# Forgetting attention with the gate sums in the mask, two heads' scores in alternating order, and squares on ScalarE

## The chip, the core and the metric

The kernel runs on one core of a Trainium2 chip. The metric is device time in microseconds, from the start of the program to its end, taken over several runs. A change is also looked at through a profile of one execution, which lists every instruction of the engines: PE (TensorE) with its weight loads PEld, DVE (VectorE), ACT (ScalarE), POOL (GpSimd), and SP, whose queue issues the DMA transfers.

## The reference

A model of four layers for one sequence of 256 tokens and width 1024 in float32. The first layer puts 16 meta tokens in front (272 positions) and mixes them by two groups of eight attention heads each, MLA (latent) and forgetting attention. The change concerns the forgetting heads, whose mathematics is this (B = 1, dimension 64, causal):

```
qf = rms_norm(fq, g_q_fox);  kf = rms_norm(fk, g_k_fox);  vf = fv
log_f = log_sigmoid(f_logit + b_forget)
F = cumsum(log_f over positions)                # one sum per head and position
s[q, k] = qf[q] . kf[k] * 64**-0.5 + F[q] - F[k]
p = softmax(where(k <= q, s, -1e30));  o = p @ vf
```

F[q] is the same for all keys of a query, so it falls out of the softmax; -F[k] does not. All other layers (a short convolution, a differential attention, an mLSTM, four squared-ReLU MLPs) are the same in both kernels.

## The kernel before, in words

**Stream and precision.** All weight matrices lie in one stream of 128x128 tiles. `Weights._ensure` (L82 to L100) loads 16 tiles (1 MB) at a time into one of three buffers `raw` on SP's queue (L86), and splits four tiles at a time into a rounded part `whi` on ACT (L92) and a rest `wlo` on DVE (L95; while `shared` is set, every third on POOL). `mm3` (L176) does each product as three f32r matmuls (L179 to L181). A matmul whose operands are plain f32 is issued as two instructions.

**Order.** [...] `queue_behind` (L67) adds an order between two instructions without a wait. [...]

**The attention layer** (`attention`, L343). `latent_proj` and `latent_norm` (L358, L375) make the two latents; `latent_norm` squares its chunks on POOL (L380) and adds them there (L384), sums over partitions on PE (L385), and applies the inverse root on DVE (L391) before a split into the operands `g_ckv` and `g_cq`. A mixed group gives the shared rotary key `kp` (its square `sqpe` L416 and its scaling L417, both on POOL) and the forget logits, from which `log_sigmoid_setup` and a scan (L424) make `cum`, the sums F as 8 rows of 272. L426 to L440 build from it the operands of a gate product: `fq` (F in two parts and ones, in 32-row groups), `fk` (ones and -F) and `hot` (one-hot columns), zeros elsewhere.

`fox_groups` (L449) projects the forgetting queries and keys, two heads to a tile of 128 rows: copy out of PSUM on ACT (L454), square on POOL (L456), gain on POOL (L458). `fox_norm` (L460) sums the squares per head by L464 on PE and writes the inverse roots to DRAM; `fox_scale` (L670) reads them back broadcast and multiplies on POOL (L676). Three of the eight tiles come early (at 34 to 47 us), five after the MLA queries. The MLA keys get their norm through DRAM as well: `kapd` (L490), then a broadcast for each head (`kt`, L515), on SP's queue; L649 needs them.

`minis` (L560) treats the last two meta tokens as queries (2 rows, 16 keys); `pair(j, ...)` (L595) treats the 256 others for the heads 2j and 2j + 1. For each head e a PSUM bank from a pool of two (`stile`) takes two score blocks, 128 queries by 144 keys and 128 by 272. `v.tensor_tensor_reduce` (L612) adds the causal mask, scales and takes the extreme; ACT takes the exponential (L615); DVE normalises (L617 to L621); PE transposes (L623 to L625); ACT copies (L627); the products with the values (L637, L641, L642) go into one bank, the two heads in its two halves of 64 partitions; `split` makes the operands of the output projection. The projection's first half needs the MLA heads only and lies between the forgetting pairs; the second half follows them.

The scores differ by group. MLA has L649 and L650 over 128 rows. For a forgetting head `fox_mm` (L652) adds two products in PSUM: L654 over the head's 64 rows (rows 0 to 63 for even heads, 64 to 127 for odd ones) and L655, the gate product over 128 rows with `fkh`, which is `fk` masked to this head on POOL (L662). For the small scores the masked copy is `fkm` (L667).

Of the kernel before, what the change touches and what calls it, by code (L numbers as in the profile page):

```python
# [6 lines left out]
F32 = mybir.dt.float32  # L7
F32R = mybir.dt.float32r
AF = mybir.ActivationFunctionType
# [5 lines left out]
P = 128  # L15
# [51 lines left out]
def queue_behind(tc, later, earlier):  # L67
# [3 lines left out]
        reason="issue order")  # L71

# [53 lines left out]
class Model:  # L126
# [216 lines left out]
    def attention(self, hv):  # L343
        with ExitStack() as c2:
# [30 lines left out]
            def latent_norm(cs, gain, n):  # L375
                nch = len(cs)
                pst = self.xtile(n)
                for c in range(nch):
                    q = self.tmp("latsq", n, width=T)
                    g.tensor_tensor(out=q, in0=cs[c], in1=cs[c], op=ALU.mult)  # L380
# [35 lines left out]
            g.tensor_tensor(out=sqpe[64:], in0=kp[64:], in1=kp[64:], op=ALU.mult)  # L416
            g.tensor_tensor(out=kp[64:], in0=kp[64:], in1=tabk[64:], op=ALU.mult)  # L417
# [8 lines left out]
            fq = ap.tile([P, T], F32R, name="fq")  # L426
            fk = ap.tile([P, T], F32, name="fk")
            hot = ap.tile([P, 8], F32, name="hot")
            g.memset(fq.bitcast(F32), 0.0)
            g.memset(fk, 0.0)  # L430
            g.memset(hot, 0.0)
            for r in (0, 32, 64, 96):
                g.tensor_copy(hot[r:r + 8], ident[0:8, 0:8])
            for r in (0, 32):
                g.tensor_copy(fk[r:r + 8], self.onesrow)
                g.tensor_copy(fq[64 + r:72 + r], self.onesrow)
            v.tensor_copy(fq[0:8], cum)
            v.tensor_tensor(out=fq[32:40], in0=cum, in1=fq[0:8].bitcast(F32), op=ALU.subtract)
            for r in (0, 32):
                v.tensor_scalar(out=fk[64 + r:72 + r], in0=fq[r:r + 8].bitcast(F32), scalar1=-1.0, scalar2=None, op0=ALU.mult)  # L440
# [8 lines left out]
            def fox_groups(js):  # L449
                for j in js:  # L450
# [3 lines left out]
                    s.activation(out=fraw[j], in_=pt, func=AF.Copy)  # L454
                    fsq[j] = self.tmp("sq8", n, bufs=8, width=T)
                    g.tensor_tensor(out=fsq[j], in0=fraw[j], in1=fraw[j], op=ALU.mult)  # L456
                    gain = self.vec("gk_fox") if j >= 4 else self.gqf8
                    g.tensor_scalar(out=fraw[j], in0=fraw[j], scalar1=gain, scalar2=None, op0=ALU.mult)  # L458
# [101 lines left out]
            def minis(score, scale, banks):  # L560
# [6 lines left out]
                for e in range(2):  # L567
# [6 lines left out]
                    else:  # L574
                        v.tensor_copy(sv[:, :, e], pm_)
# [17 lines left out]
            mask = self.cst("maskb")  # L593

            def pair(j, score, scale, vals, mini, oc):  # L595
# [6 lines left out]
                px = []  # L602
# [54 lines left out]
            def score_fox_mini(dst, h):  # L657
                fox_mm(dst, h, 14, 16, 16, fkm[:, h])
# [654 lines left out]
```

## Time and profile before

| | us |
|---|---|
| median of 3 runs (1237.07 to 1240.48) | 1238.38 |
| the profiled execution, its own time | 1238.09 |
| span of that execution, first to last instruction | 1236.3 |
| PE busy / PEld busy | 1214.4 / 1166.9 |
| DVE busy / ACT busy / POOL busy | 890.6 / 740.0 / 175.0 |

The granted TensorE clock is 0.997 of full speed in the mean. Busy times are shares of the whole span, over stages with different limits. Matmuls are pipelined, so the distance from one start to the next tells more of what one costs than its listed duration does. A merged row of the time line (x2, x4) has the first start and the time from there to the last end. What ended an idle time is inferred from semaphore events.

### The profile page before, as it was taken

The page shows a single profiled execution, that of the slowest core. Times are in us where ns is not written, and L with a number is a line of the kernel's source. Part 1 is how long each engine was busy: PE and PEld are TensorE (multiplying, and loading weights), DVE is VectorE, ACT ScalarE, POOL GpSimd, SP SyncE. Part 2 cuts the span into 40 slices and gives each one's busy share as a digit, 9 for nine tenths or more (in the row PEclk, how much of TensorE's full clock was granted, in tenths as well). Part 3 has the DMA queues.
Part 4 walks back from the last instruction along what each step waited for, and adds up shares of the span by engine and source line. Part 5 has one row for each costly group of instructions (what it writes and reads, how often), then busy time and mean ns, then how long its engine had stood idle before and what let it go on. Part 6 is the DMA issues. An engine that isn't in the chain of part 4 may idle for free.

```text
span 1236.3 us, 24763 instructions
## 1 busy us (share of the span) xinstructions
PE 1214.4 (98%) x9628; PEld 1166.9 (94%) x9628; DVE 890.6 (72%) x1792; ACT 740.0 (60%) x1518; POOL 175.0 (14%) x218
## 2 busy tenths in 40 slices
PE   8999999999999999999999999999999999999996
PEld 7787789999999999999998999999999989999996
DVE  7786668766567787766557888776558888876553
ACT  5655557764555567755446666775447665776452
POOL 5543330001101120001001011000100313000110
PEclk9999999999999999999999999999999999999998
DMA  7343126545455454554564435555555534554551
GB/s 279 121 173 105 52 98 219 182 174 200 172 178 197 171 196 181 181 195 171 189 212 147 156 118 184 192 175 190 183 179 186 184 135 157 189 200 171 189 187 35
DMA packets 35417, 210.15 MB, mean 170 GB/s; under 512 B 4642, under 2 KB 9940, under 8 KB 10852
## 3 DMA queue, kind: packets, MB, share of 16 engines
q1 hardware_dynamic: 34628, 207.98, 47.8%
q8 instruction: 76, 1.25, 0.4%
q10 hardware_dynamic: 576, 0.52, 0.1%
q14 instruction: 41, 0.34, 0.1%
q0 software_dynamic: 96, 0.06, 0.0%
HBM read 207.45 MB, written 1.10 MB: 169 GB/s over the span
## 4 chain that ended last, share of the span: by engine, by line
PE 93%; DVE 4%; DMA 1%; ACT 1%; issue 0%; POOL 0%; SPq 0%; DVEq 0%; ACTq 0%
PE d L179 26%; PE d L180 26%; PE d L181 26%; PE s L179 1%; DVE wlo L95 1%; PE s L180 1%; PE s L181 1%; PE d L336 1%; PE d L337 1%; PE d L338 1%; PE s L654 1%; DVE xl L201 1%; DMA kapd<-row 0%; PE y L179 0%; DVE ht L317 0%
## 5 line engine op out<-in xcount | busy, mean ns | idle before, releaser
L92 ACT ACTIVATE whi<-raw 128x512 fp32r<-128x512 f32 x768 | 478.7, 630 | 361.3 <-PE d L180 320.8
L95 DVE TENSOR_TENSOR wlo<-raw,whi 128x512 fp32r<-128x512 f32 x763 | 540.0, 713 | 211.6 <-ACT whi L92 194.5
L180 PE MATMUL d<-xl,whi 128*128 128x256 f32 (+2 forms) x1472 | 418.1, 285 | 2.4 <-DVE xl L201 2.4
L179 PE MATMUL d<-xh,whi 128*128 128x256 f32 (+2 forms) x1472 | 416.9, 284 | 2.0 <-DVE ht L317 1.6
L181 PE MATMUL d<-xh,wlo 128*128 128x256 f32 (+2 forms) x1472 | 414.1, 282 | 0.0
L181 PE MATMUL d<-uh,wlo 128*128 128x256 f32 (+1 forms) x1024 | 289.9, 283 | 0.0
L179 PE MATMUL d<-uh,whi 128*128 128x256 f32 (+1 forms) x1024 | 289.6, 283 | 0.0
L180 PE MATMUL d<-ul,whi 128*128 128x256 f32 (+1 forms) x1024 | 289.3, 282 | 0.0
L180 PEld LDWEIGHTS d<-xl,whi 128*128 128x128 f32 x1472 | 277.8, 189 | 4.7 <-DVE xl L201 3.0
L179 PEld LDWEIGHTS d<-xh,whi 128*128 128x128 f32 x1472 | 277.3, 189 | 5.2 <-ACT whi L92 2.9
L181 PEld LDWEIGHTS d<-xh,wlo 128*128 128x128 f32 x1472 | 279.1, 190 | 1.1 <-issue 0.3
L179 PEld LDWEIGHTS d<-uh,whi 128*128 128x128 f32 x1024 | 196.1, 191 | 0.0
L180 PEld LDWEIGHTS d<-ul,whi 128*128 128x128 f32 x1024 | 196.1, 191 | 0.0
L181 PEld LDWEIGHTS d<-uh,wlo 128*128 128x128 f32 x1024 | 195.6, 191 | 0.0
L252 POOL TENSOR_TENSOR acc<-ht 128x256 f32<-128x256 f32 (+1 forms) x8 | 5.3, 663 | 449.6 <-DVE ht L317 449.6
L260 POOL TENSOR_TENSOR acc<-sq,acc 128x256 f32<-128x256 f32 (+1 forms) x48 | 44.8, 934 | 139.7 <-ACT sq L257 137.8
L198 DVE TENSOR_TENSOR ul<-q,uh 128x256 fp32r<-128x256 f32 (+1 forms) x128 | 54.1, 425 | 11.5 <-ACT uh L197 0.2
L304 DVE SCALAR_TENSOR_TENSOR u<-d,rs 128x256 f32<-128x256 f32 (+1 forms) x116 | 48.9, 424 | 18.1 <-PE d L181 17.7
L197 ACT ACTIVATE uh<-q 128x256 fp32r<-128x256 f32 (+1 forms) x128 | 53.0, 416 | 3.4
L306 ACT ACTIVATE q<-u 128x256 f32<-128x256 f32 (+1 forms) x128 | 52.7, 415 | 0.0
L317 DVE TENSOR_TENSOR ht<-d,ht 128x256 f32<-128x256 f32 (+1 forms) x74 | 30.3, 420 | 18.8 <-PE d L181 18.8
L201 DVE SCALAR_TENSOR_TENSOR xl<-ht,vecs,xh 128x256 fp32r<-128x256 f32 (+2 forms) x64 | 41.2, 654 | 0.3 <-ACT xh L200 0.3
(425 smaller groups left out, 1516.9 us busy)
## 6 DMA issues: line engine op xcount, KB each, us to landing
raw<-in_wstream_dram SPq DMA_DIRECT2D x191, 1024.0 KB, 4.8
ht<-in_xt_dram SPq DMA_DIRECT2D x8, 136.0 KB, 4.0
kt<-kapd SPq DMA_DIRECT2D x8, 136.0 KB, 3.5
raw<-in_wstream_dram SPq DMA_DIRECT2D x4, 256.0 KB, 4.3
bt<-brd SPq DMA_DIRECT2D x8, 128.0 KB, 3.3
consts<-in_consts_dram SPq DMA_DIRECT2D x1, 556.0 KB
fbc<-kfd SPq DMA_DIRECT2D x8, 68.0 KB, 2.6
fbc<-kfd SPq DMA_DIRECT2D x8, 64.5 KB, 2.7
```

Source lines behind the costliest of these rows:

```text
L92: a = nc.scalar.activation(out=self.hi, in_=src, func=AF.Copy)
L95: b = e.tensor_tensor(out=self.lo, in0=src, in1=self.hi.bitcast(F32), op=ALU.subtract)
L179: te.matmul(pt, wh, ah, start=first, stop=False)
L180: te.matmul(pt, wh, al, start=False, stop=False)
L181: te.matmul(pt, wl, ah, start=False, stop=last)
L197: self.s.activation(out=out_h, in_=src, func=AF.Copy)
L198: self.v.tensor_tensor(out=out_l, in0=src, in1=out_h.bitcast(F32), op=ALU.subtract)
L201: self.v.scalar_tensor_tensor(out=out_l, in0=src, scalar=scale, in1=out_h.bitcast(F32), op0=ALU.mult, op1=ALU.subtract)
L260: self.g.tensor_tensor(out=self.acc, in0=sq, in1=self.acc, op=ALU.add)
L304: self.v.scalar_tensor_tensor(out=u, in0=pt, scalar=0.0, in1=rs, op0=ALU.max, op1=ALU.mult)
L306: self.s.activation(out=q, in_=u, func=AF.Square)
L317: self.v.tensor_tensor(out=hv[m], in0=pt, in1=hv[m], op=ALU.add)
```

## The change

The gate product goes. The rows F are written to DRAM (`cumd`) once; for each head `gate_mask` broadcasts its row to 128 partitions on SP's queue and subtracts it on POOL from the causal mask, for both blocks, into one of three buffers `fmk`; L612's successor adds this in place of the plain mask. The small scores subtract `gate2`, loaded once, where there was a copy. `pair` takes both PSUM banks first and has both heads' scores issued at once; `score_fox` does block 144 of both heads and then block 272 of both, in a fixed order (`queue_behind`), and makes the first one wait for the last reduction issued before (`starts_after`). The products with the values go by key block and then head instead of head and then block. The latents' squares, `sqpe` and the forgetting squares move from POOL to ACT, the latter now straight out of PSUM; the forgetting gain goes into ACT's copy; `kp`'s scaling moves to DVE.

```diff
@@ -69,6 +69,14 @@
         reason="issue order")
...
+def starts_after(tc, later, earlier):
...
+    tc.add_manual_dep(
+        later.ins, earlier.ins.name,
+        mybir.DependencyInfo(mybir.DependencyClass.Sync, mybir.DependencyReason.DATA),
+        reason="both banks free")
@@ -377,7 +385,7 @@
                     q = self.tmp("latsq", n, width=T)
-                    g.tensor_tensor(out=q, in0=cs[c], in1=cs[c], op=ALU.mult)
+                    s.activation(out=q, in_=cs[c], func=AF.Square)
                     if c == 0:
@@ -413,8 +421,8 @@
             sqpe = ap.tile([P, T], F32, name="sqpe")
-            g.tensor_tensor(out=sqpe[64:], in0=kp[64:], in1=kp[64:], op=ALU.mult)
-            g.tensor_tensor(out=kp[64:], in0=kp[64:], in1=tabk[64:], op=ALU.mult)
+            s.activation(out=sqpe[64:], in_=kp[64:], func=AF.Square)
+            v.tensor_tensor(out=kp[64:], in0=kp[64:], in1=tabk[64:], op=ALU.mult)
             krp = self.xtile(T)
@@ -423,21 +431,9 @@
-            fq = ap.tile([P, T], F32R, name="fq")
-            fk = ap.tile([P, T], F32, name="fk")
-            hot = ap.tile([P, 8], F32, name="hot")
-            g.memset(fq.bitcast(F32), 0.0)
-            g.memset(fk, 0.0)
-            g.memset(hot, 0.0)
-            for r in (0, 32, 64, 96):
-                g.tensor_copy(hot[r:r + 8], ident[0:8, 0:8])
-            for r in (0, 32):
-                g.tensor_copy(fk[r:r + 8], self.onesrow)
-                g.tensor_copy(fq[64 + r:72 + r], self.onesrow)
-            v.tensor_copy(fq[0:8], cum)
-            v.tensor_tensor(out=fq[32:40], in0=cum, in1=fq[0:8].bitcast(F32), op=ALU.subtract)
-            for r in (0, 32):
-                v.tensor_scalar(out=fk[64 + r:72 + r], in0=fq[r:r + 8].bitcast(F32), scalar1=-1.0, scalar2=None, op0=ALU.mult)
...
+            cumd = self.dp.tile([8, T], F32, name="cumd")
+            self.nc.sync.dma_start(cumd, cum)
@@ -451,11 +447,9 @@
                     fraw[j] = ap.tile([P, n], F32, name=f"fqk{j}")
-                    s.activation(out=fraw[j], in_=pt, func=AF.Copy)
                     fsq[j] = self.tmp("sq8", n, bufs=8, width=T)
-                    g.tensor_tensor(out=fsq[j], in0=fraw[j], in1=fraw[j], op=ALU.mult)
-                    gain = self.vec("gk_fox") if j >= 4 else self.gqf8
-                    g.tensor_scalar(out=fraw[j], in0=fraw[j], scalar1=gain, scalar2=None, op0=ALU.mult)
+                    s.activation(out=fsq[j], in_=pt, func=AF.Square)
+                    s.activation(out=fraw[j], in_=pt, func=AF.Copy, scale=self.vec("gk_fox") if j >= 4 else self.gqf8)
@@ -557,7 +551,7 @@
-            def minis(score, scale, banks):
+            def minis(score, scale, banks, gate=None):
                 sm_ = ap.tile([2, 4, 2, 32], F32, tag="mini_s", name="mini_s")
@@ -572,7 +566,7 @@
                     else:
-                        v.tensor_copy(sv[:, :, e], pm_)
+                        v.tensor_tensor(out=sv[:, :, e], in0=pm_, in1=gate[:, :, e], op=ALU.subtract)
                 mx = ap.tile([2, 4, 2], F32, tag="mini_m", name="mini_m")
@@ -591,26 +585,28 @@
             mask = self.cst("maskb")
...
-            def pair(j, score, scale, vals, mini, oc):
+            self.last_reduce = None
...
+            def pair(j, score, scale, masks, vals, mini, oc):
                 vd, vt = vals
...
                 g.memset(pn, 0.0)
-                px = []
                 pTs = []
+                scs = [self.stile(), self.stile()]
+                score(scs, j)
                 for e in range(2):
                     h = 2 * j + e
-                    sc = self.stile()
-                    score(sc, h)
+                    sc = scs[e]
+                    mk = masks(h)
                     pe_ = self.tmp("pexp", 416, bufs=3)
...
                         c = 2 * e + i
-                        v.tensor_tensor_reduce(
-                            out=dst, in0=sc[:, o:o + n], in1=mask[:, T - n:], scale=scale(h, i), scalar=3.0e38,
+                        self.last_reduce = v.tensor_tensor_reduce(
+                            out=dst, in0=sc[:, o:o + n], in1=mk[i], scale=scale(h, i), scalar=3.0e38,
                             op0=ALU.add, op1=ALU.min, accum_out=mn[:, c:c + 1])
@@ -625,7 +621,6 @@
                     s.activation(out=pT, in_=x[:, 0:384], func=AF.Copy)
-                    px.append(x)
                     pTs.append(pT)
@@ -635,37 +630,49 @@
                 te.matmul(po, vd[:, j * P:j * P + P], p0, start=True, stop=False)
-                for e in range(2):
-                    cs = slice((2 * j + e) * 64, (2 * j + e) * 64 + 64)
-                    pe2 = po[64 * e:64 * e + 64]
-                    te.matmul(pe2[:, 2:], vt[:, 0, cs], pTs[e][:, 0:256], start=False, stop=False)
-                    te.matmul(pe2[:, 130:], vt[:, 1, cs], pTs[e][:, 256:], start=False, stop=True)
+                for i, (o, ks) in enumerate(((2, slice(0, 256)), (130, slice(256, 384)))):
+                    for e in range(2):
+                        cs = slice((2 * j + e) * 64, (2 * j + e) * 64 + 64)
+                        te.matmul(po[64 * e:64 * e + 64, o:], vt[:, i, cs], pTs[e][:, ks], start=False, stop=i == 1)
                 self.split(oh[oc], ol[oc], po)
...
-            def score_mla(sc, h):
-                te.matmul(sc[:, 0:144], QT[h][:, 2:130], KT[h][:, 0:144], start=True, stop=True)
-                te.matmul(sc[:, 144:416], QT[h][:, 130:], KT[h], start=True, stop=True)
...
-            def fox_mm(dst, h, q0, q1, n, fkh):
+            def score_mla(scs, j):
+                for e in range(2):
+                    h = 2 * j + e
+                    te.matmul(scs[e][:, 0:144], QT[h][:, 2:130], KT[h][:, 0:144], start=True, stop=True)
+                    te.matmul(scs[e][:, 144:416], QT[h][:, 130:], KT[h], start=True, stop=True)
...
+            def fox_mm(dst, h, q0, q1, n):
                 r = 64 * (h % 2)
-                te.matmul(dst, fraw[h // 2][r:r + 64, q0 - NM:q1 - NM], fraw[4 + h // 2][r:r + 64, 0:n], start=True, stop=False)
-                te.matmul(dst, fq[:, q0:q1], fkh[:, 0:n], start=False, stop=True)
+                return te.matmul(dst, fraw[h // 2][r:r + 64, q0 - NM:q1 - NM], fraw[4 + h // 2][r:r + 64, 0:n], start=True, stop=True)
...
             def score_fox_mini(dst, h):
-                fox_mm(dst, h, 14, 16, 16, fkm[:, h])
...
-            def score_fox(sc, h):
-                fkh = self.tmp("fkh", T, bufs=2, dt=F32R)
-                g.tensor_scalar(out=fkh, in0=fk, scalar1=hot[:, h:h + 1], scalar2=None, op0=ALU.mult)
-                fox_mm(sc[:, 0:144], h, 16, 144, 144, fkh)
-                fox_mm(sc[:, 144:416], h, 144, T, T, fkh)
...
-            fkm = ap.tile([P, 8, 16], F32R, name="fkm")
-            g.tensor_tensor(out=fkm, in0=fk[:, 0:16].unsqueeze(1).to_broadcast([P, 8, 16]),
-                            in1=hot.unsqueeze(2).to_broadcast([P, 8, 16]), op=ALU.mult)
+                fox_mm(dst, h, 14, 16, 16)
...
+            def score_fox(scs, j):
+                before = None
+                for o, n, q0 in ((0, 144, 16), (144, T, 144)):
+                    for e in range(2):
+                        mm = fox_mm(scs[e][:, o:o + n], 2 * j + e, q0, q0 + P, n)
+                        if before is not None:
+                            queue_behind(self.tc, mm, before)
+                        elif self.last_reduce is not None:
+                            starts_after(self.tc, mm, self.last_reduce)
+                        before = mm
...
+            def gate_mask(h):
+                mk = self.tmp("fmk", 416, bufs=3)
+                fb = mk[:, 144:]
+                sync.dma_start(fb, cumd[h].partition_broadcast(P))
+                g.tensor_tensor(out=mk[:, 0:144], in0=mask[:, T - 144:], in1=fb[:, 0:144], op=ALU.subtract)
+                g.tensor_tensor(out=fb, in0=mask, in1=fb, op=ALU.subtract)
+                return mk[:, 0:144], fb
...
+            gate2 = ap.tile([2, 4, 2, 16], F32, name="gate2")
+            sync.dma_start(gate2, cumd.rearrange("(h e) t -> h e t", e=2)[:, :, 0:16].partition_broadcast(2))
@@ -680,12 +687,12 @@
             for j in range(4):
-                pair(j, score_mla, lambda h, i: rq[:, i * 8 + h:i * 8 + h + 1], vm, mini_m, j)
+                pair(j, score_mla, lambda h, i: rq[:, i * 8 + h:i * 8 + h + 1], lambda h: (mask[:, T - 144:], mask), vm, mini_m, j)
             fox_scale()
-            mini_f = minis(score_fox_mini, None, "ys")
+            mini_f = minis(score_fox_mini, None, "ys", gate2)
             vf = turned_values()
             for j in range(4):
-                pair(j, score_fox, lambda h, i: -1.0, vf, mini_f, 4 + j)
+                pair(j, score_fox, lambda h, i: -1.0, gate_mask, vf, mini_f, 4 + j)
             for c in range(8):
...
             self.W.shared = True
```

## Rows read from the trace of the kernel before

**Rows 1.** The page, busy time: us, share of the span, instructions of each engine.
```profile
PE 1214.4 (98%) x9628; PEld 1166.9 (94%) x9628; DVE 890.6 (72%) x1792; ACT 740.0 (60%) x1518; POOL 175.0 (14%) x218
```

**Rows 2.** By stretch: its us, busy of PE PEld DVE ACT POOL (instructions), clock, DMA, GB/s.
```profile
50.00:100.00 50.00, 48.92 (x353) 40.91 (x352) 38.05 (x122) 28.08 (x75) 14.89 (x20) 1.00 0.36 131
...
120.00:130.00 10.00, 10.00 (x61) 7.26 (x60) 5.87 (x27) 5.52 (x18) 4.55 (x4) 1.00 0.31 107
130.00:140.00 10.00, 10.00 (x64) 7.91 (x63) 6.99 (x34) 6.08 (x21) 4.44 (x6) 1.00 0.31 105
140.00:150.00 10.00, 10.00 (x65) 7.17 (x65) 7.47 (x35) 5.93 (x21) 0.19 (x1) 1.00 0.01 2
150.00:160.00 10.00, 10.00 (x63) 7.46 (x63) 0.98 (x3) 3.06 (x8) 1.27 (x1) 1.00 0.31 105
```

**Rows 3.** Instructions in order of time, PE, one forgetting head: start, us, line, tiles, shape, count.
```profile
123.98 0.40 PE L180 MATMUL d<-ol,whi 128*128 128x258 f32 x2
124.32 0.51 PE L654 MATMUL s<-fqk,fqk 64*128 64x144 f32 x2
124.76 0.34 PE L655 MATMUL s<-fkh,fq 128*128 128x144 f32 x1
125.02 0.72 PE L654 MATMUL s<-fqk,fqk 64*128 64x272 f32 x2
...
125.90 0.28 PE L181 MATMUL d<-oh,wlo 128*128 128x258 f32 x1
```

**Rows 4.** The same view, scores of one head of the differential attention.
```profile
651.01 0.27 PE L181 MATMUL d<-xh,wlo 128*128 128x256 f32 x1
651.21 0.50 PE L820 MATMUL s<-dk,dq 64*128 64x128 f32 x4
651.54 0.61 PE L821 MATMUL s<-dk,dq 64*128 64x256 f32 x4
652.07 0.38 PE L179 MATMUL d<-xh,whi 128*128 128x256 f32 x1
652.30 0.28 PE L180 MATMUL d<-xl,whi 128*128 128x256 f32 x1
```

**Rows 5.** The same view, small scores of the forgetting heads.
```profile
114.98 0.17 PE L655 MATMUL y<-fkm,fq 128*2 128x16 f32 x1
115.08 0.20 PE L654 MATMUL y<-fqk,fqk 64*2 64x16 f32 x2
```

**Rows 6.** The same view, 46 to 88 us; in brackets idle time before and its releaser.
```profile
46.32 0.63 PE L464 MATMUL x<-sq,consts 128*16 128x272 f32 x2 [1.75 <-POOL sq L456]
47.03 0.62 PE L485 MATMUL x<-sq,consts 128*8 128x272 f32 x2
47.58 0.39 PE L179 MATMUL d<-g_cqh,whi 128*128 128x258 f32 x1
...
87.37 0.61 PE L464 MATMUL x<-sq,consts 128*16 128x258 f32 x2 [0.43 <-POOL sq L456]
```

**Rows 7.** The same view, ACT, a square out of PSUM.
```profile
47.24 0.40 ACT L480 ACTIVATE sq<-d 128x272 f32<-128x272 f32 x1
```

**Rows 8.** Groups by line and form, POOL, 0 to 200 us: busy, mean ns, idle before.
```profile
L662 POOL TENSOR_SCALAR fkh<-fk,hot 128x272 fp32r<-128x272 f32 x8 | 8.5, 1065 | 12.5 <-PE s L655 10.3 <-PE d L180 2.2
...
L676 POOL TENSOR_TENSOR fqk<-fbc,fqk 128x272 f32<-128x272 f32 x4 | 3.2, 800 | 2.3 <-DMA fbc<-kfd 1.7 <-PE d L181 0.6
```

**Rows 9.** The chain that ended last, in order of time: start, us, what.
```profile
55.40 5.36 DMA kapd<-row
60.77 2.88 DMA kt<-kapd
```

**Rows 10.** Instruction groups by line, DVE, 121 to 160 us.
```profile
L612 DVE CUSTOM_DVE_ANT_0 pexp<-s,consts 128x144 f32<-128x144 f32 (+1 forms) x16 | 5.4, 372 | 7.6 <-PE s L655 6.9 <-PE x L625 0.7
```

**Rows 11.** The chain again, two pairs' products with the values.
```profile
140.45 0.59 PE y L641 x4
...
158.26 0.58 PE s L641 x2
```

## The prediction

> **What bounds the kernel now.** I read the page's busy line first: PE has work for 1214.4 us of a span of 1236.3, the other engines far less [rows 1]. So time taken off PE counts in full where PE is dense, and work put on another engine costs only where that engine makes PE wait. Next the busy time by stretch, for the stage the change touches: from 120 to 160 us PE is busy throughout, while DVE has 21.3 and ACT 20.6 us of work in those 40; before it, from 50 to 100 us, ACT has 22 us of 50 free [rows 2]. The reader is to see that the forgetting pairs run under a full PE with room on DVE and ACT. Then PE's instructions in order of time show what one head's scores cost, and PE's idle gaps with what ended them show where GpSimd holds PE up.
>
> **The scores.** A head now has two blocks (144 and 272 columns), each an f32 product over 64 rows (two passes, L654) and a gate product over 128 rows (L655). In the row of two L180, 0.40 us long for passes of 0.28, the second starts 0.12 later, at 124.10; its place ends at 124.22, and the next ordinary product starts at 125.90 [rows 3]. One head costs 1.68 us, eight cost 13.4.
>
> After the change a pair of heads has four 64-row products and no gate product, and the heads alternate between rows 0 to 63 and 64 to 127. The kernel has this form already, in the differential attention: L820 and L821 are two maps on the two halves of the rows. There, the last L181 starts at 651.01, so its place ends at 651.13; L179 starts at 652.07 and its follower only 0.23 later instead of 0.12. The block of four costs (652.07 - 651.13) + 0.11 = 1.05 us, of which 0.86 lies between the first start at 651.21 and L179 [rows 4]. These have 128 + 256 columns, ours 144 + 272: 0.86 x 416/384 + 0.19 = 1.12 us a pair, 4.5 us for four. If the heads did not overlap, a pair would cost what rows 3 show for the f32 products alone, 2 x (0.44 + 0.65) = 2.18 us (124.32 to 124.76, and 0.72 less the same 0.07 of tail), 8.7 in all. I take the overlap, since rows 4 are the same shape of work in the same kernel: **13.4 - 4.5 = 8.9 us off PE**, with 4.7 as the lower end and 9.7 as the upper, if the 0.19 at a pair's edges went too.
>
> **The small scores of the last two meta tokens.** Eight gate products go, each 0.10 us from its start to the next start [rows 5]: **0.8 us**.
>
> **Squares and scalings off GpSimd.** PE stands 1.75 us before L464 at 46.32 and 0.43 us before the one at 87.37, both for a square on POOL [rows 6]. Both squares move to ACT, where one takes 0.40 us from PSUM [rows 7], and the gain goes into the copy that exists already. The upper end is 2.2 us. But what comes next is near: after that L464 PE waits for L485's square on ACT and reaches g_cq at 47.58 [rows 6], behind g_cq's own normalisation. That also comes forward, because its squares leave GpSimd, and DVE loses the four small operations that built fq and fk and gains one. I take **1.5 us**; the lower end is 0. The 14 squares now on ACT are 14 x 0.40 = 5.6 us, spread over the stages before the pairs, where ACT has room like the 22 us free in 50 to 100. Without that cover, whi would be late and PE would stand.
>
> **The masks.** Each head gets a 136 KB broadcast on SP's queue and two subtractions on GpSimd. The nearest rows: a two-input operation of 128x272 there takes 0.80 us (L676), the one-input fkh that goes 1.07 [rows 8]; with 144 columns at 0.80 x 144/272 = 0.42 a head costs 1.22 against 1.07, eight 9.8 against 8.5, beside PE. [...] Three masks can be ready early. From the fourth on, one waits until the reduction of the head three earlier has read its buffer, then for landing (2.9 us for kt's broadcast [rows 9]) and GpSimd (1.2): 4.1 us, against 7 to 8 us from pair to pair (31 us for four, below). It should hide; if not, a pair can wait all of it. I take 0, ends 0 and 4 x 4.1 = 16.4.
>
> On SP, the sums' write, three masks and the small gate load stand in one queue with the weights and with kapd. The kapd chain (5.36 us, then 2.88) stands on the chain that ended last [rows 9], so a transfer waiting ahead of kapd would be paid for directly. The sums come out of the same early stage as the latents, well ahead of the keys' norm in the program, so I take 0.
>
> **The wait put ahead of a pair.** The first score waits for the last reduction of the pair before. Behind it in PE's queue stand the projection's products. DVE's reductions are themselves late mostly because of PE: 6.9 of their 7.6 us of idle time end with L655 [rows 10], so they come forward with the scores. The stage from 120 to 160 shrinks from 40 us to about 31, with 21.3 us of DVE's work in it [rows 2]; for the tail of the last pair I take 0.5 us of PE time, ends 0 and 4.5 (half the scores' gain).
>
> **The products with the values** alternate heads too. Most pairs run that way now (four L641 in 0.59 us); others run apart, each head's two taking 0.58 [rows 11]. Three of eight pairs do; tying them would give 3 x (2 x 0.58 - 0.59) = 1.7 us. Nothing in the edit forces that when the second head is late, so I take 0, ends 0 and 1.7.
>
> **Sum.** 8.9 + 0.8 + 1.5 - 0.5 = 10.7 us. The profiled execution took 1238.09 us, 0.29 below the median of the runs, so 1238.1 - 10.7 = **1227.4 us**. A measurement of this kernel can tell about 0.3%, 3.7 us, from no change.
>
> **The rivals.**
> - The stage becomes bound by the chain through DVE and ACT instead of PE. For it: DVE and ACT at 6 to 7.5 of 10 us up to 150 before PE is relieved, and only the first half of the projection as filler. Against it: DVE is nearly idle from 150 to 160, so it had room at the end [rows 2]. Half of the scores' gain goes: 1227.4 + 4.5 - 0.5 = 1231.4. Chance 0.2.
> - The change does not do what it says: the two heads' products run one after another, or something is put between them. Rows 4 speak against it. The gain falls by 4.2: 1231.6. Chance 0.08.
> - Slower: the masks set the pace. Each pair waits a whole round of a mask (reduction, SP, landing, subtraction), 4.1 us, and so does kapd once for the sums' landing, 5.36 us: 16.4 + 5.4 - 10.7 = 11 us slower, 1249. It turns slower once the waits exceed 10.7 us, some 2.7 us for each pair. For it: SP's queue is in order and weight loads wait long in it. Against it: three buffers, and a round shorter than a pair. Chance 0.05; a further 0.07 that two pairs wait, 8.2 us, 1235.6.
>
> **How the numbers follow.** The forecast has 0.6 (its own range 1223.7, every upper end: 9.7 + 0.8 + 2.2 + 1.7 = 14.4, to 1229, nothing from L464). The first two rivals lie below 1234.4, where 'faster' ends, but for 0.03 that I leave them beyond it. Faster 0.85, same 0.10, slower 0.05. The range reaches from 1223.7 to 1234.5, over the first two rivals, and leaves out about 0.15.
>
> **What would show it.** In the changed profile: L655's place gone; from the product ahead of a forgetting pair to the one behind it about 1.1 us, with starts of both heads some 0.01 us apart; no PE idle before the fox squares' L464; DVE's reductions waiting for PE, not for POOL; PE 100% in the stage, which ends some 11 us earlier (about 159 to 148). Wrong if DVE's reductions wait for GpSimd's mask or a DMA, if PE shows idle time ahead of the forgetting scores, if kapd's issue moves late, or if stages after 170 us change their own lengths.

## The result, and the profile after

| | us |
|---|---|
| after, median of 4 runs (1225.07 to 1226.38) | 1225.78 |
| before, its runs beside them, median | 1238.55 |
| ratio, 95% interval | 0.9898 (0.9884 to 0.9912) |
| profiled execution of after, its own time / span | 1225.74 / 1224.0 |
| after once more in the last batch, median of 5 (1227.30 to 1229.53) | 1228.89 |
| its ratio | 0.9916 (0.9903 to 0.993) |

Faster by 0.8 to 1.0%, 1227.4 forecast. That the same kernel took 3 us longer in the last batch is itself a finding, taken up below. The profiled spans differ by 12.3 us (1236.3 to 1224.0), the busy time of PE by 11.7 (first row here against [rows 1]). From the start of the output projection's last product to the end of the span it is 1069.1 us before and 1068.5 after. These 0.7 us lie behind VectorE's last operation, 4.16 and 3.50 us from the end; the changed kernel and all its variants have the shorter end (1068.3 to 1068.5), and no step of the prediction had it.

The page's busy line of after, then its stretches as in [rows 2]:

```profile
PE 1202.7 (98%) x9604; PEld 1159.8 (95%) x9604; DVE 888.0 (73%) x1789; ACT 743.5 (61%) x1532; POOL 141.9 (12%) x191
```
```profile
120.00:130.00 10.00, 9.63 (x80) 8.68 (x78) 9.86 (x40) 6.02 (x20) 4.28 (x7) 1.00 0.51 147
130.00:140.00 10.00, 8.74 (x58) 5.48 (x56) 8.00 (x41) 7.84 (x29) 5.39 (x8) 1.00 0.25 43
140.00:150.00 10.00, 9.03 (x68) 7.39 (x69) 3.45 (x15) 4.36 (x14) 0.19 (x1) 1.00 0.22 93
150.00:160.00 10.00, 8.41 (x68) 8.03 (x68) 10.00 (x17) 7.48 (x18) 9.83 (x12) 1.00 0.31 112
```

PE, full here before, now has holes, and DVE has 9.86 us of work in the first ten. What ended PE's waits, from the view of waits (113 to 150 us: total, times, longest):

```profile
PE d L187 <- ACT oh L205: 2.2, 3, 1.0
PE y L629 <- DVE pn L617: 0.4, 1, 0.4
```

Three times PE stands at the second half of the projection, which needs the pairs' output `oh`: the first half has run out. PE's instructions in order of time show two of the four pairs, as [rows 3] showed a head:

```profile
122.74 0.28 PE L189 MATMUL d<-oh,wlo 128*128 128x258 f32 x1
122.96 0.97 PE L650 MATMUL s<-fqk,fqk 64*128 64x144 f32 x8
123.86 0.39 PE L187 MATMUL d<-oh,whi 128*128 128x258 f32 x1
...
129.36 0.97 PE L650 MATMUL s<-fqk,fqk 64*128 64x144 f32 x6
130.25 0.33 PE L619 MATMUL x<-consts,pexp 128*128 128x128 f32 x1
130.51 0.72 PE L650 MATMUL s<-fqk,fqk 64*128 64x272 f32 x2
131.17 0.33 PE L620 MATMUL x<-consts,pexp 128*128 128x128 f32 x1
```

Where a pair is whole it costs what [rows 4] promised: 0.90 from its start to the next, with 0.1 more on each side, 1.1 us. Pair 2 has a transpose between its products and takes 0.90 + 0.65; pair 0 runs in two pieces, 0.44 + 0.90. Pair 3 is whole, but PE has nothing to do behind it:

```profile
134.02 0.97 PE L650 MATMUL s<-fqk,fqk 64*128 64x144 f32 x8
135.96 0.63 PE L187 MATMUL d<-oh,whi 128*128 128x258 f32 x3 [0.96 <-ACT oh L205]
```

The same view where [rows 6] had PE waiting; the first line is of before, the product ahead of its longer wait:

```profile
43.49 1.08 PE L464 MATMUL x<-sq,consts 128*16 128x272 f32 x4
```

```profile
42.37 0.62 PE L479 MATMUL x<-sq,consts 128*8 128x272 f32 x2
42.83 1.54 PE L458 MATMUL x<-sq,consts 128*16 128x272 f32 x6
44.20 0.62 PE L479 MATMUL x<-sq,consts 128*8 128x272 f32 x2
44.75 0.39 PE L187 MATMUL d<-g_cqh,whi 128*128 128x258 f32 x1
```

All three early squares now run without a wait between them, and `g_cq` begins 2.8 us earlier (47.58 to 44.75); 1.4 of that is the earlier start of the whole stage, see below. Last, the groups of DVE (113 to 150 us) and of POOL (0 to 200), as in [rows 10] and [rows 8]:

```profile
L617 DVE TENSOR_SCALAR pn<-pexp,rc 128x16 f32<-128x16 f32 x16 | 5.5, 342 | 0.0
...
L608 DVE CUSTOM_DVE_ANT_0 pexp<-s,fmk 128x144 f32<-128x144 f32 (+1 forms) x16 | 5.1, 366 | 1.5 <-POOL fmk L671 1.5
```
```profile
L671 POOL TENSOR_TENSOR fmk<-consts,fmk 128x272 f32<-128x272 f32 x8 | 6.5, 820 | 0.1
...
L670 POOL TENSOR_TENSOR fmk<-consts,fmk 128x144 f32<-128x144 f32 x8 | 4.5, 565 | 25.3 <-DMA fmk<-cumd 21.9 <-DVE ht L325 2.8 <-DVE pn L617 0.5
```

**Where the time went.** For each PE instruction I take the time from its start to the next one's start and add these up by tile, from the first product of `g_ckv` to the last of the output projection (39.95 to 167.17 us before, 38.55 to 155.50 after). PE's four waits among the forgetting pairs stand in a row of their own: what the instruction ahead of each takes beyond its like elsewhere, 1.03 us behind pair 3's scores, 0.94 and 0.54 behind transposes, 0.56 behind the last value product (listed as idle: 0.96, 0.78, 0.37 and 0.49).

| TensorE time, us | before | after | difference |
|---|---|---|---|
| gate products (`fkh`) | 3.43 | 0 | -3.43 |
| big 64-row scores, with four small ones | 9.25 | 5.22 | -4.03 |
| other small scores with their gates | 1.03 | 0.28 | -0.75 |
| sums of squares (`sq`), with two waits before | 8.68 | 6.01 | -2.67 |
| value products, forgetting / MLA | 4.79 / 4.01 | 3.20 / 3.77 | -1.83 |
| transposes of `pexp` and `pn` | 6.04 | 5.84 | -0.20 |
| the four waits | 0 | 3.07 | +3.07 |
| all else | 89.99 | 89.56 | -0.43 |
| sum | 127.22 | 116.95 | -10.27 |

The start lies a further 1.4 us earlier (39.95 to 38.55), but that is no gain of the edit: in the second profile of the same kernel it lies at 40.02. PE's passes of 272 columns come 0.23 us apart until 8.3 us in the first profile and until 11.1 in the second and in the kernel before; from then on they come 0.12 to 0.13 apart. In the first profile and in the kernel before, the granted clock reads 1.00 on both sides of that step, so what sets the early pace is not shown.

### The profile page after: what moved, and what is told of

Read it like the earlier page. It is cut to its first block, busy times and chain, and to the rows that moved or that the text cites. A ratio compares the mean times of both kernels' runs of the same rounds, so it can differ in the third digit from the quotient of the medians.

```text
span 1224.0 us, 24712 instructions
## 1 busy us (share of the span) xinstructions
PE 1202.7 (98%) x9604; PEld 1159.8 (95%) x9604; DVE 888.0 (73%) x1789; ACT 743.5 (61%) x1532; POOL 141.9 (12%) x191
## 4 chain that ended last, share of the span: by engine, by line
PE 95%; DVE 3%; ACT 1%; DMA 0%; issue 0%; POOL 0%; DVEq 0%; SPq 0%; POOLq 0%; ACTq 0%
PE d L187 27%; PE d L188 26%; PE d L189 26%; PE d L344 1%; PE s L187 1%; PE d L345 1%; PE s L188 1%; PE s L189 1%; PE d L346 1%; DVE wlo L103 1%; DVE xl L209 0%; PE x L252 0%; PE y L187 0%; PE y L188 0%; DVE ht L325 0%; PE y L189 0%
## 5 line engine op out<-in xcount | busy, mean ns | idle before, releaser
L268 POOL TENSOR_TENSOR acc<-sq,acc 128x256 f32<-128x256 f32 (+1 forms) x48 | 44.9, 935 | 139.4 <-ACT sq L265 137.5
```

What stands on the lines that cost most here:

```text
L268: self.g.tensor_tensor(out=self.acc, in0=sq, in1=self.acc, op=ALU.add)
```

## The experiments

Ratios are to the kernel before on the same chip. The last column is the length of the attention stage in the one profiled execution, from the first product of `g_ckv` to the last of the output projection, as in the sum above (127.22 before, 116.95 in the changed kernel's first profile). What lies ahead of it varies with the early pace (38.55 and 40.02 us in the changed kernel's two profiles), what lies behind it does not, so it tells more of the variants than medians that differ by 1 or 2 us; but it is one execution each, and the changed kernel's own two differ by 2.2 us, for reasons taken up below. Lines in the edits are those of the kernel named.

| run | median us (runs) | ratio, 95% interval | stage, us |
|---|---|---|---|
| squares alone, on the kernel before | 1235.0 (10) | 0.9979 (0.9969 to 0.9988) | 125.57 |
| squares back on GpSimd | 1231.73 (4) | 0.9944 (0.9929 to 0.9959) | 118.13 |
| scores head by head | 1227.35 (4) | 0.9925 (0.9901 to 0.9949) | 117.16 |
| heads apart | 1227.12 (4) | 0.9908 (0.9894 to 0.9922) | 117.92 |
| value products head by head | 1228.24 (4) | 0.9914 (0.9899 to 0.9929) | 118.14 |
| seven masks early | 1225.98 (4) | 0.9905 (0.9891 to 0.992) | 116.30 |
| no wait for both banks | 1225.58 (4) | 0.9904 (0.9887 to 0.992) | 115.95 |
| small scores in another bank | 1227.97 (4) | 0.9908 (0.9892 to 0.9925) | 121.40 |
| turned values between the pairs | 1225.85 (4) | 0.9895 (0.988 to 0.991) | 115.82 |
| the same, beside the changed kernel | 1225.92 (4) | 0.9897 (0.9884 to 0.9911) | 115.94 |
| the changed kernel again | 1228.89 (5) | 0.9916 (0.9903 to 0.993) | 119.18 |
| values between, masks early, no wait | 1225.33 (4) | 0.9895 (0.9882 to 0.9909) | 115.70 |

### What the squares are worth

The first run puts the hunks of L380, L416 and L454 to L458 alone into the kernel before; the second takes them back out of the changed one.

```diff
-                    g.tensor_tensor(out=fsq[j], in0=fraw[j], in1=fraw[j], op=ALU.mult)
...
+                    s.activation(out=fsq[j], in_=pt, func=AF.Square)
...
```

> The kernel before with only the squares and scalings moved from GpSimd (latents, shared rotary key, forgetting heads); gate products, head order and masks stay. The prediction's term: 1.5 us, at most 2.2, so about 1237. Theory after the first reading of the two traces: the move is worth more, since PE reaches the first latent query product 2.8 us earlier and the two stalls on L464 go (2.2 us), so 3 to 4 us: 1235. Rival: what the changed kernel has won ahead of the projection (5.3 us) comes from the regrouped scores of the MLA pairs and the small scores, then this run stays within 1.5 us of before.

Measured 2.7 us (1237.69 to 1235.0; 1.5 to 3.8 by the interval), and TensorE's sums of squares fall to 6.08 us as in the changed kernel: the whole of that row of the table comes from this part.

> The changed kernel, with all squares and scalings back on GpSimd (the other parts of the change stay). Theory S (the parts add up: the squares moved alone into the kernel before were worth 2.7 us): 2.2 to 3.2 us slower than the changed kernel, 1228 to 1229. Rival H (what is won ahead of the forgetting stage is partly eaten by waits that the other parts bring): 0.5 to 1.8 us slower, 1226.3 to 1227.6. Rival G (GpSimd now also makes the masks, so squares and masks queue behind each other): over 4 us slower, above 1229.8.

Measured about 5.7 us against the changed kernel's first ratio (3.5 against its second), more than rival G's mark, but not for its reason. The rotary product waited, at 37 us, long before any pair. From the time lines of POOL, first in the kernel before and then in this run, and of PE, and the stretches:

```profile
31.46 0.64 POOL L416 TENSOR_TENSOR sqpe<-qsq 64x272 f32<-64x272 f32 x1
```
```profile
31.50 4.76 POOL L424 TENSOR_TENSOR sqpe<-qsq 64x272 f32<-64x272 f32 x1 [0.92 <-DVE qsq L420]
36.34 1.10 POOL L425 TENSOR_TENSOR qsq<-qsq,tabk 64x272 f32<-64x272 f32 x1
```
```profile
37.49 0.94 PE L427 MATMUL x<-qsq,consts 64*128 64x272 f32 x2 [2.71 <-POOL qsq L425]
```
```profile
38.00:40.00 2.00, 2.00 (x8) 1.64 (x8) 1.14 (x2) 0.39 (x1) 1.82 (x2) 0.50 0.83 342
40.00:42.00 2.00, 2.00 (x13) 2.00 (x12) 0.53 (x1) 1.03 (x2) 0.06 (x1) 0.68 0.05 14
```

One square of 64x272 on POOL took 4.76 us beside a busy DVE, PE stood 2.71 us, and then the granted clock was at 0.50 of full from 38 to 40 us and at 0.68 from 40 to 42: PE paid for the wait and again behind it. In the kernel before the same square took 0.64 us, with DVE busy there too, so what stretched it is not shown. The first product of `g_ckv` starts at 44.03 us, 4.0 to 5.5 later than in the changed kernel's two profiles, and that is most of the loss. The sums of squares take 6.01 us as in the changed kernel: the waits that the squares alone had removed did not come back. The stage is 1.2 us longer than in the first profile, with the clock low once more (0.57 from 147 to 151 us). So the two runs do not add up: undoing a part in the new surroundings is another experiment than doing it in the old ones.

### What ties two heads

The first run emits both blocks of one head and then both of the other; the second issues each head's scores ahead of its own softmax, as the kernel before did; the third does the value products head by head.

```diff
-                for o, n, q0 in ((0, 144, 16), (144, T, 144)):
-                    for e in range(2):
+                for e in range(2):
+                    for o, n, q0 in ((0, 144, 16), (144, T, 144)):
```
```diff
-                scs = [self.stile(), self.stile()]
-                score(scs, j)
...
+                    if scs[e] is None:
+                        scs[e] = self.stile()
+                        fox_mm(scs[e][:, 0:144], h, 16, 16 + P, 144)
+                        fox_mm(scs[e][:, 144:416], h, 144, 144 + P, T)
```

> The changed kernel with the four 64-row products of a pair in the order head 0 (144, 272), head 1 (144, 272) instead of alternating; same products, same waits. If the overlap of the two halves of the rows is what makes them cheap, a pair costs about 2.2 us on PE instead of 1.1, 4 us in all, of which the stalls of this stage may swallow some: 1.5 to 4 us slower than the changed kernel. If the order does not matter: within 0.5 us.

> The changed kernel with the forgetting scores issued head by head, each ahead of its own softmax, as the kernel before does; masks, squares and value products stay. In the program's order six of the eight heads then have other work around them; head 1 of pair 0 and head 0 of pair 1 still stand next to each other. Theory A (what ties two products is standing next to each other on different rows): those two run side by side, the other six heads cost some 0.9 us each, TensorE's scores 6.5 us where the changed kernel has 5.5, and the time is 0.5 to 1.5 us longer. Rival R (TensorE is not what bounds the stage, and a head that comes earlier starts its chain earlier): no loss, within 0.4 us, or up to 1 us faster.

> The changed kernel, with the value products issued head after head, as the kernel before issues them, instead of alternating. Theory A (two 64-column products run side by side when the two heads' products stand next to each other, in whatever order within the four): within 0.5 us of the changed kernel, 1225.3 to 1226.3, and the blocks at 13 to 14 ns a row pair as now. Theory B (the alternation itself ties them): the value products of the pairs cost 1.6 us more on TensorE in the forgetting stage and 0.8 a pair in the stage before, 1226.8 to 1228.5.

Scores head by head, one head of a pair that does not come together and a pair that does; then heads apart, the one place where two heads still adjoin (119.38) and a head by itself (123.47):

```profile
115.45 0.97 PE L650 MATMUL s<-fqk,fqk 64*128 64x144 f32 x4
116.35 0.39 PE L188 MATMUL d<-ol,whi 128*128 128x258 f32 x1
...
123.94 0.98 PE L650 MATMUL s<-fqk,fqk 64*128 64x144 f32 x8
124.85 0.39 PE L189 MATMUL d<-oh,wlo 128*128 128x258 f32 x1
```
```profile
119.38 0.98 PE L657 MATMUL s<-fqk,fqk 64*128 64x144 f32 x8
120.29 0.39 PE L187 MATMUL d<-oh,whi 128*128 128x258 f32 x1
...
123.47 0.97 PE L657 MATMUL s<-fqk,fqk 64*128 64x144 f32 x4
124.37 0.39 PE L188 MATMUL d<-ol,whi 128*128 128x258 f32 x1
```

Eight passes of two heads take 0.98 us, four of one head 0.97. In both runs the program has the first head's four passes ahead of the second's, yet the records start in pairs, 123.943 and 123.957, 124.170 and 124.183: all four passes of 144 columns, the second head's two among them, come before the first of 272 columns (124.292). So the alternating order is not what ties two heads; standing next to each other on the two halves of the rows is. And where other work stands between them (two of the four pairs with the scores head by head), each head costs 0.90 us, the price of a whole pair.

The value products tell the same: issued head by head, the forgetting pairs' still start 13 to 14 ns apart (6 to 7 when alternating) and take 3.23 us where alternating ones took 3.20, both without the waits behind them. That run's time, 1228.24, lies 0.7 us from the changed kernel's second median, and PE waits as in that one's profile (2.8 us in three times), so theory A holds by the trace, though its time does not stand within 0.5 of the first median. The scores head by head took 1227.35, 1.6 us above the first median and 1.5 below the second. By the first median alone that would be the forecast for heads that are not tied; the trace has 5.93 us of scores against 5.22, since two of its pairs have work between the heads, and a stage only 0.2 us longer.

Heads apart cost TensorE 1.6 us more scores than the changed kernel (6.82 against 5.22), as theory A has it: 0.90 for each of six heads and 0.91 for the two that adjoin. Part of that comes back, since PE's listed waits fall from 2.6 to 1.2 us. Its median is 1.3 us above the changed kernel's first and 1.8 below its second, and its stage 1.0 us longer than in the first profile, so rival R's "no loss" is not borne out.

### Masks and the wait

```diff
-                mk = self.tmp("fmk", 416, bufs=3)
-                fb = mk[:, 144:]
+                if 3 <= h <= 6:
+                    ma, fb = self.tmp("sq8", 144, bufs=8, width=T), self.tmp("sq8", T, bufs=8)
...
```
```diff
-                        elif self.last_reduce is not None:
-                            starts_after(self.tc, mm, self.last_reduce)
```
```diff
-            mini_f = minis(score_fox_mini, None, "ys", gate2)
+            mini_f = minis(score_fox_mini, None, "d", gate2)
```

> The changed kernel with buffers enough that the masks of seven heads are made ahead of the forgetting pairs (heads 3 to 6 in buffers that the squares have left). Theory: the stage lost some 4 to 5 us of its gain, of which DVE's waits for masks (1.5 us) and DVE operations stretched beside GpSimd's subtractions (about 2.7 us) are the larger part; then this run is 2 to 4 us faster than the changed kernel. Rival: the stage is short of filler and bound by the chain through DVE and ACT whatever the masks do; then within 0.7 us.

> The changed kernel without the wait of a pair's first score for the last reduction of the pair before (the order of the four products stays). If the wait holds PE up: 0.5 to 2 us faster. If it keeps the two heads together: 0.5 to 2 us slower, with the first head's block standing alone. If the planned order is the same anyway: within 0.5 us.

> The changed kernel, with the small scores of the forgetting attention in another bank, so that the first pair finds both of its score banks free. Rival R (the first pair's split head, 3.5 us between its two heads, costs its overlap and delays all that follows): 0.6 to 1.5 us faster than the changed kernel, 1224.3 to 1225.2, first pair's four products side by side in about 1.1 us. Theory T (TensorE is short of other work in this stage, so that what the first pair saves is waited away later): the first pair is tied but the time stays within 0.5 us, 1225.3 to 1226.3.

The first two leave the time where it was (1225.98 and 1225.58). The masks are no bound by themselves: with seven of them ready, DVE no longer waits 1.5 us for them, and PE still waits elsewhere (2.0 us). Without the forced wait all of PE's waits go but the last (0.49 us), though no work was moved. But two more pairs are split: the 64-row products of the four pairs take 5.76 us where the changed kernel has 4.70 without its wait. So both answers of the expectation are true at once: the wait holds PE up, and it keeps two heads together. The stage is 1.0 us shorter for it (115.95); it began 0.5 us later in that execution, and the median is only 0.2 us lower.

The third is inconclusive. Its first pair is split all the same (0.44 and 0.90 us). Another bank changed the order of the MLA stage too, PE waited there, and the granted clock fell to 0.50 from 100 to 102 us; later PE stood 1.43 us at the forced wait, and the clock was low again (0.51 from 140 to 147). The profile is also of the slowest of its four executions (1231.39).

### Whether work is lacking in the stage

The three transposes that turn a pair's values move from before all pairs to just before their own pair. One further kernel has this with the early masks and without the wait.

```diff
             for j in range(4):
+                chunk(j)
                 pair(j, score_fox, lambda h, i: -1.0, gate_mask, vf, mini_f, 4 + j)
```

> The changed kernel, with the turned values of the forgetting attention made pair by pair: the chunk of four transposes for pair j stands just before pair j, where all four chunks stood before pair 0. TensorE's sum of work is the same; some of it moves into the stage. Theory T (the gain in the forgetting stage is cut because the chain of a pair through VectorE and ScalarE is longer than the work TensorE has beside it, so that it runs out of the first half's projection and then waits): the moved transposes fill waits, 2 to 3.5 us faster than the changed kernel, 1222.3 to 1223.8, and TensorE's waits on the output halves (tile oh) near 136, 140 and 148 us shrink. Rival R (the waits are set by the order of the pairs and their banks, whatever work there is beside them): no gain, 1225.3 to 1227, with the waits still there.

> The changed kernel itself, unaltered, to have its time beside the three that follow. Expected: 1225.0 to 1226.5 (1225.78 before), TensorE waiting about 2 us in the forgetting stage.

> The turned values made pair by pair, once more, beside the changed kernel: the first time the waits of TensorE in the stage went, and the stage was 1.2 us shorter in the one trace, but the median did not move. Theory P (the waits are worth their full length once other work stands in them, and only the scatter hid it): 0.8 to 1.5 us faster than the changed kernel of the same batch. Theory Q (the passes moved into the waits add as much time at the edges of the 64-row products as they save): within 0.4 us of it.

> Three alterations of the changed kernel at once: turned values pair by pair, seven masks ready ahead, and no wait of a pair's first score for the reduces of the pair before. Theory P: 1 to 2 us faster than the changed kernel of the same batch, since every wait seen in the stage's trace has lost its cause. Theory Q: within 0.5 us, the stage staying at 44.5 to 45.5 us from the first turned value to the last value product, filled with TensorE's work from end to end.

Stretches and waits of the second run with values between:

```profile
115.00:130.00 15.00, 15.00 (x119) 12.76 (x117) 14.63 (x55) 10.31 (x34) 6.87 (x10) 1.00 0.45 150
130.00:140.00 10.00, 10.00 (x70) 7.26 (x67) 8.24 (x26) 6.21 (x20) 4.53 (x6) 1.00 0.25 70
```
```profile
PE d L187 <- ACT oh L205: 0.5, 1, 0.5
```

PE is full again; of the three waits one of 0.5 us is left, after the last pair. Both times the kernel took 1225.9 us: as the changed kernel in its first batch, 3.0 us less than in the last, and the three together 3.6 less. So theory T's 2 to 3.5 us did not come against the first median and did come against the second. By the stage the gain is 1.0 to 1.1 us (115.82 and 115.94 against 116.95), with the three together 1.2, since here too all four pairs are split and their scores take 5.76 us, not 4.70: theory P has the waits right and theory Q the edges. With the three together it is 44.9 us from the first turned value to the last value product, as theory Q said, where the changed kernel's first profile has 46.1.

That the moved work filled the waits is not shown. It is three transposes a pair, some 0.3 us, and the order of PE's other work changed with it: the first half of the projection ends 22.6 us after its first product instead of 20.2. The run without the forced wait ends the same waits with nothing moved, and has the same stage.

What differs stands in the changed kernel's second profile. Its waits, DVE and POOL in order of time, and its stretches:

```profile
PE d L187 <- ACT oh L205: 2.8, 3, 1.3
```
```profile
136.27 0.35 DVE L616 TENSOR_SCALAR pexp<-pexp,rc 128x256 f32<-128x256 f32 x1
...
137.94 1.55 DVE L616 TENSOR_SCALAR pexp<-pexp,rc 128x256 f32<-128x256 f32 x1
```
```profile
137.95 1.27 POOL L103 TENSOR_TENSOR wlo<-raw,whi 128x512 fp32r<-128x512 f32 x1
```
```profile
142.00:144.00 2.00, 1.37 (x7) 0.90 (x9) 1.71 (x9) 1.51 (x6) 0.00 (x0) 1.00 0.67 283
144.00:146.00 2.00, 2.00 (x13) 1.50 (x12) 0.43 (x1) 0.48 (x2) 0.00 (x0) 0.56 0.04 8
146.00:148.00 2.00, 2.00 (x13) 2.00 (x12) 0.00 (x0) 0.56 (x2) 0.00 (x0) 0.58 0.00 0
```

The same scaling took 0.35 us and, beside GpSimd's `wlo`, 1.55. In the first profile it was done (136.21 to 136.56) before that `wlo` began at 136.86. PE's wait grew from 1.05 to 1.59 us between starts, and behind the waits the granted clock fell: 0.56 and 0.58 of full over 4 us, where the first profile has 1.00 from 96 to 156 us. From the third pair's first value product to the last pair's last it is 7.40 us here and 5.85 there. With 1.5 from the clock, 0.5 from the wait and 1.5 from the later start (40.02 against 38.55), the 3.8 us between the two executions (1225.74 and 1229.53) are nearly accounted for. Only this one of the five executions was traced: two others took 1227.3 and two 1228.9 and 1229.1, which would fit, and is not shown.

The run with the value products head by head parts the two effects. Its DVE and PE:

```profile
137.29 1.55 DVE L616 TENSOR_SCALAR pexp<-pexp,rc 128x256 f32<-128x256 f32 x1
```
```profile
141.98 0.62 PE L187 MATMUL d<-oh,whi 128*128 128x258 f32 x3 [1.32 <-ACT oh L205]
```

It has the same stretched scaling and the same longer wait, but the granted clock stays at 1.00 behind it. So the stretched scaling goes with the longer wait in both traces, while a wait of this length does not by itself bring the clock down; what decides that is open.

## Why the prediction was right, and where not

The time was forecast at 1227.4; the two medians lie on either side of it, 1.6 below and 1.5 above. The mechanism was right where it took work off PE, and wrong in the step that PE stays full. That the stage's sum came out at 10.3 us, against 10.7 forecast, is luck: four of its terms were off by more than 1 us each, two either way.

- **The scores: 8.9 forecast, 7.5 measured.** The mechanism was right: no gate product, two heads side by side, 1.1 us for a whole pair. Both ends of the subtraction were off. From start to start the eight heads before cost 12.16 us (3.43, and 8.73 for the big 64-row products), a mean of 1.52: four were whole at 1.59 (1.68 with the 0.09 of entering that the one head I read has in it), four already split at 1.37 to 1.49. After it is 4.70 us without the wait behind pair 3, not 4 x 0.90, since two pairs are split and take 1.34 and 1.55. The prediction had something put between the heads as a rival for the whole stage; it came for half of it.
- **The small scores: 0.8 forecast, 0.75 measured**, 1.55 us to 0.80; the four of them in the table's second row took 0.52 before and after.
- **The squares: 1.5 forecast, 2.7 measured**, above my upper end of 2.2, which counted two waits as the view of waits lists them. Counted from start to start, these two and a short one ahead of L485 are 2.7 us, all of the row's gain; the six passes stood next to each other before too, but for the wait. What I took off for the work that comes next was not lost: PE reaches `g_cq` without a wait.
- **The value products: 0 forecast, 1.8 measured**, a little above its upper end. Three of the eight pairs were untied before, one is now; from start to start an untied pair costs 0.78 us more than a tied one, where listed durations gave 0.57.
- **The tail and the wait: 0.5 lost forecast, 3.1 measured**, the largest error, within its ends of 0 and 4.5. Here rival (a) came true beside the forecast: the stage is bound by the chain through DVE and ACT, and the first half of the projection runs out, as the rival said. The prediction's "PE 100% in the stage" failed: 9.63, 8.74 and 9.03 of 10. Without the forced wait for both banks PE's waits go, but for the last, and the stage is 1.0 us shorter although more pairs are split; with the values between the pairs they go too, the forced wait still there, so which part of the order brings them is open. The clock that falls behind the waits in some executions had no step at all.
- **The masks: 0 forecast.** As a queue they cost nothing that shows in the time (seven early: 1225.98). One sign of being wrong did appear, in small: DVE's reductions waited for GpSimd's mask, 1.5 us in all. The slower rival fell: no pair waited a round of a mask, and `kapd` was issued at 52.2 us, not 55.4. The 1.22 us a head (0.80 + 0.42) measured 0.82 + 0.57 = 1.39.

The scores and the tail gave 4.0 us less than forecast, the squares and the value products 3.0 more, and the rows that no step had 0.6 more. The profiled execution shows 12.3 us because 1.4 of earlier start and 0.7 at the program's end come on top of the stage's 10.3.

## What to carry to other kernels

Work taken off a full engine is worth its length only until something else becomes the chain: here some 13 us went off TensorE's stage and 3 came back as waits. Give the waits a row of their own when you add up a stage; spread over the instructions ahead of them they made a gain of 7.5 us in the scores look like 6.4. Cost a shape from start to start over all of its places, not over one, because here half of them were split. An order that is forced to keep two products together had a price here: without it more of them were split, and the stage was still shorter (115.95 against 116.95 us). And a stage whose main engine had just got waits lost clock on top of them in one of its two traced executions (0.56 and 0.58 of full over 4 us); the version with the values between the pairs is no faster than the changed kernel's first runs, but took the same time in both of its batches.

## What the runs showed of the hardware

- Two 64-row products on the two halves of the rows ran side by side even where the program has one head's whole block first: eight passes in 0.98 us, four in 0.97, and the second head's passes of 144 columns start (by 124.183) ahead of the first head's of 272 (124.292).
- VectorE's scaling of 128x256 from SBUF to SBUF took 1.55 us instead of 0.35 in two traces, in the changed kernel's second one beside GpSimd's `wlo` (two inputs, 128x512, 1.27 us). In the first profile three of the reductions L608, which read PSUM and a mask, kept their 0.30, 0.44 and 0.31 us beside a `wlo` of 1.30. What in the two operations makes the difference, the traces do not show.
- The granted clock fell behind a few waits of 0.4 to 1.3 us in one execution and not in another of the same program, whose longest wait there was 0.96 us: 0.56 and 0.58 of full from 144 to 148 us, where the other has 1.00, and passes 0.214 us apart instead of 0.12, from 144.3 to 147.6 us. In the run with the value products head by head it stayed at 1.00 behind the same waits, 1.32 us the longest; with the squares back on GpSimd and with the small scores in another bank it fell behind waits of 1.32 and 1.43 us, to 0.57 and 0.51.
